# Hybrid DiT step in split fp32: loads and products of the start reordered, the last unit's second stream in two fresh banks, later gate rows and residual, other tables

## The chip, the cores and the metric

The kernel runs on one core of one Trainium2 chip. The metric is the device time in microseconds of one execution. A core has five engines that run their own instruction streams side by side: TensorE (PE, matrix products into PSUM banks), VectorE (DVE), ScalarE (ACT), GpSimd (POOL) and SyncE (SP, which here issues most DMAs). They wait for each other by semaphores.

## What is computed

One layer of a diffusion backbone for 128 prompt tokens and 128 sample tokens, model width 2048, all in fp32:

```python
shift1, scale1, gate1, shift2, scale2, gate2 = split(silu(c) @ w_ada + b_ada, 6)   # adaLN, per stream
h  = rms_norm(x) * (1 + scale1) + shift1
qa, ka, va, qb, kb, vb, ga, gb = split(h @ w_in)                                   # 2048 x 8704
oa = window_gqa(qa, ka, va, cache_a)       # 8 heads of 128, 2 key/value heads, rotary, QK-norm
ob = neighbourhood(qb, kb, vb, cache_b)    # 8 heads of 128, 2-D bias, QK-norm
m  = (sigmoid(ga) * (oa @ w_br_a) + sigmoid(gb) * (ob @ w_br_b)) @ w_out
x  = x + gate1 * m
h2 = rms_norm(x) * (1 + scale2) + shift2
y  = x + gate2 * (relu(h2 @ w_up) ** 2 @ w_down)                                   # inner width 8192
```

The new keys and values of the prompt are outputs too.

## The kernel before

**Products.** Every fp32 operand is split into a high part, which the engine multiplies in one pass, and a low rest; a product is the sum of three matmuls, high x high, high x low and low x high (L467 to L469 and L340 to L342, and L1408 to L1410 in the fast pairs). ACT makes a weight's high part by a copy (L108). The low part is made in one of two ways: DVE subtracts the high part from the raw weight (L268), or `minus_plus` (L274, L275) lets ACT write the negative of the high part and POOL issue a DMA that adds the raw weight from memory onto it. Tables choose the second way: `LO_DMA` for plain weights (wL), `XL_DMA` and `YL_DMA` for two halves of a fast pair (XL, YB); their keys are step numbers, or 8 times the piece plus the place in it.

**Steps.** The weights go by in steps of 512 KB (128 x 1024 values): SP loads a step into a buffer `raw` (L239), ACT and DVE split it, PE multiplies it in 12 matmuls of 512 columns, six for each of the two token streams (0 is the prompt, 1 the sample), into two PSUM banks. A unit is a run of steps that ends in one pair of banks, 512 output columns wide. `run()` walks all steps; at each it issues loads, splits and products so many steps ahead as the tables `RUN`, `LOOK` and `AHEAD` say. Other work is hung onto steps by tables (`ADA_AT`, `JOBS`, `POST`, `DOTS`, `T_PAIR` and more).

**The start.** The first five steps are written out by hand in `begin()` (L530 to L690): their loads go in halves of 256 KB (`k` is the half), between the loads of the first two adaLN pairs (`pair_load`, L349). The rest of the adaLN products goes through `mod_pairs`: groups 1 to 6 of eight loads each (`araw`) and their products (`ps_ada`, L358), at the steps in `ADA_AT`.

**Attention.** Probabilities are transposed either by PE (L963, for the entries of `TE`) or by DMA.

**The MLP.** The up-projection runs in pieces; where `FAST` names them, pairs of blocks go through a scheme with one product fewer, on sums of blocks (`up_pair`, L1408 to L1521). The down-projection's partial sums of a piece wait in `dsum`, some of them in memory (`DS_AWAY`), and are put back into a bank by ACT.

**The end.** The last unit of all is `last_unit` (L1338): for its last two steps it computes stream 0 first, evacuates it (`out_s`: DVE multiplies by the gate rows, L1138, and adds to the residual x1b, L1142; SP stores), and then finishes stream 1, its last step in two halves of 256 columns in the same bank. The gate rows g2 and the residual (`gate_bc`, `x1_back`) are loaded ahead, six steps before the end of a unit of the piece before the last.

Of the kernel before, what the change touches and what calls it, by code (L numbers as in the profile page):

```python
# [32 lines left out]
SILU_AT = 6  # L33
FB_DVE = 6
FB1 = 14
H_AT = 42
DOTS1 = [19, 26, 29, 33, 34, 34, 40, 42]
# [12 lines left out]
BEGIN_SEED = ()  # L50
FAST = {1: (0, 1, 3, 7), 2: (0, 2, 4, 7), 3: (0, 3, 4, 5, 7), 4: (0, 2, 4, 6, 7), 5: (0, 1, 3, 6, 7), 6: (0, 1, 3, 6, 7), 7: (0, 2, 3, 5, 7)}
AWAY = [('gB', 2), ('gB', 0), ('gA', 0)]
GATE_BACK = 7
SEED_IN = {3: 0, 4: 1}
SEED_AT = 4
DIRECT = (3,)
LO_DMA = {123: 3, 162: 4, 196: 6, 205: 8, 233: 5, 421: 5, 452: 5}

LOOK = "220102342600004321112333333423344346003343323264425550024766435445100474621316521154444204744421242145443452135211233544444376555544342442445533113321545566643343457745545676631233475557402456897561133345442776554653214434322546645533234767635734543210333332754523544642203425555547355455542235444454346622143243143533120323340312252123324443413423323622444434555345666437402100223322544523544524557200014130212545432212544243022242111444300005772000137786"
RUN = "143538999224623021111226444342023133100001316655554435733333554564563325525103544635357136486300020025420321354421003432333255533612243352667454523663311454555543535997565577799967554203545745166866764795556988745674676472100044367288985999944454243112133555665422126411011224421346635244575533444454353423332446683456501300223410454545542322431521552123100123853233511252576696622311441202144625734434231022445134778334434464132124568676567978669999987788"  # L60
AHEAD = "822111111111101110000000111111110000000000122222221000000000000011122211000020133110000100000233100000000000002200000000000001112000000000000111000000100000000000000000011100000011111232221244332110000000000000000000000003011311110000000002000000000001020000000000000000000000000000002220001100100000000000000000000000000100000000000000001000222222222322320000000000000000000010000000000100000000000000000000000000000211110000000100000000012444242132345400"
CONST_AT = [63, 75]
XL_DMA = {9: 0, 11: 11, 16: 0, 20: 8, 23: 6, 26: 0, 29: 0, 36: 0, 37: 0, 38: 0, 43: 0, 46: 5, 53: 0, 54: 0, 63: 0}
ADA_G = ((1,), (2,), (3, 4), (5, 6))
ADA_AT = [None, 5, 14, 20, 22, 37, 38]
# [8 lines left out]
DOTS2 = [222, 233, 234, 234, 235, 238, 245, 247, 254, 265, 269, 270, 272, 288, 300, 301, 304, 327, 328, 331, 333, 336, 349, 359, 360, 362, 364, 368, 393, 393, 395, 401]
STAT_AT = [4, -1, 9, 3]
T_PAIR = [[12, 6], [6, 10], [5, 10], [6, 10], [6, 10], [6, 10], [7, 12]]
P_PAIR = [[3, -1], [2, 4], [3, 3], [1, 4], [2, 5], [1, 5], [2, 0]]
# [9 lines left out]
def tile_hybrid_step(ctx: ExitStack, tc: tile.TileContext, a):  # L87
# [10 lines left out]
    def G(name, dt=F32):  # L98
        return gp.tile([P, 1024], dt, name=name, tag="g")
# [427 lines left out]
    def begin():  # L527
# [21 lines left out]
        def lo(j, k):  # L549
            prep_lo(sts[j], k)  # L550
# [65 lines left out]
        for j in range(2, n):  # L616
            banks(j)
            if 3 < j + 1 < n:
                hi(j + 1, 0)
                lo(j + 1, 0)  # L620
            if j == n - 2:
                mod_q(1, 2)
            by_stream(j, 0, 0)
            if j == n - 2:
                mod_q(1, 3)
                ada_evac(mb[1], 256)
            if j == n - 1:
                first_h(1)
                hi(1, 1)
            keep(j, 0)  # L630
            by_stream(j, 0, 1)
            if j == n - 2:
                ada_cols(mb[1], 0, 1, 1)
                hi(0, 1)
                lo(0, 1)
            keep(j, 1)
# [701 lines left out]
    def last_unit(w, c0, ktiles, stat, evac_s, key, seed_from=None):  # L1338
# [207 lines left out]
    def down_unit(p, n):  # L1546
# [261 lines left out]
```

## Time and profile before

| | before |
|---|---|
| median of 3 runs | 1321.33 us (1320.77 to 1322.04) |
| the profiled run | 1321.1 us, span 1319.3 us |
| PE busy | 1306.7 us, 99% of the span |
| DVE busy | 1123.5 us, 85% |
| ACT busy | 905.1 us, 69% |
| moved by DMA | 400.12 MB, mean 303 GB/s |

The span is the profiled time from the first to the last instruction. An engine's busy time counts overlapping matmuls once. PE's clock was granted in full in all of the 40 slices of the page.

### The profile page before, as it was taken

How to read it: one execution, taken by the hardware profiler on the slowest of the kernel's cores; microseconds unless marked ns; L12 is line 12 of the kernel's file. 1: busy time of each engine (PE TensorE's matmuls, PEld its weight loads, DVE VectorE, ACT ScalarE, POOL GpSimd, SP SyncE). 2: the span in 40 equal slices, each digit the busy share in tenths (PEclk: the TensorE clock that was granted, in tenths of full speed). 3: DMA queues.
4: the chain of work that ended last, by engine and by line, in shares of the span. 5: the costliest groups of instructions: out<-in, count | busy, mean ns of one | idle time of the engine just before them, and what ended most of it. 6: DMA issues, size and time to landing. Idle time of an engine off the chain costs nothing. (4 is left out here: it accounts for less than half of the span.)

```text
span 1319.3 us, 18022 instructions
## 1 busy us (share of the span) xinstructions
PE 1306.7 (99%) x6334; PEld 1057.9 (80%) x6335; DVE 1123.5 (85%) x1437; ACT 905.1 (69%) x1143; POOL 57.1 (4%) x65
## 2 busy tenths in 40 slices
PE   9999999999999999999999999999999999999998
PEld 4778778788888878888888888888888778878887
DVE  4669799988999999999788897997999899879474
ACT  5635655789866556536786868869778597787780
POOL 0000000431000000001000000000000000000000
PEclk9999999999999999999999999999999999999999
DMA  9999999998899989988798998778896886788861
GB/s 374 408 408 371 409 409 354 395 289 262 281 339 314 407 308 330 374 332 254 235 259 308 290 324 256 275 263 252 279 321 222 272 279 240 254 274 299 303 263 48
DMA packets 168939, 400.12 MB, mean 303 GB/s; under 512 B 70768, under 2 KB 72016, under 8 KB 168848
## 3 DMA queue, kind: packets, MB, share of 16 engines
q1 hardware_dynamic: 164688, 387.09, 81.3%
q0 software_dynamic: 4016, 11.80, 4.8%
q8 instruction: 49, 0.80, 0.2%
q14 instruction: 42, 0.34, 0.1%
q10 hardware_dynamic: 144, 0.08, 0.0%
HBM read 373.45 MB, written 10.80 MB: 291 GB/s over the span
## 5 line engine op out<-in xcount | busy, mean ns | idle before, releaser
L268 DVE TENSOR_TENSOR wL<-raw,wH 128x1024 fp32r<-128x1024 f32 x382 | 450.8, 1221 | 79.1 <-ACT wH L108 71.3
L108 ACT ACTIVATE wH<-raw 128x1024 fp32r<-128x1024 f32 (+1 forms) x396 | 393.2, 1040 | 107.5 <-DMA raw<-in_w_in 20.9
L467 PE MATMUL acc<-wH,hH 128*128 128x512 f32 x272 | 107.5, 395 | 0.6 <-ACT wH L108 0.6
L468 PE MATMUL acc<-wL,hH 128*128 128x512 f32 x272 | 105.9, 390 | 0.0
L469 PE MATMUL acc<-wH,hL 128*128 128x512 f32 x272 | 105.9, 389 | 0.0
L340 PE MATMUL acc<-wH,hH 128*128 128x512 f32 x252 | 100.7, 399 | 0.0
L342 PE MATMUL acc<-wH,hL 128*128 128x512 f32 x252 | 98.2, 390 | 0.0
L341 PE MATMUL acc<-wL,hH 128*128 128x512 f32 x252 | 98.2, 390 | 0.0
L1638 DVE CUSTOM_DVE_ANT_0 aT<-aT,cB,cols 128x1024 f32<-128x1024 f32 x56 | 71.5, 1283 | 0.6
L1638 DVE CUSTOM_DVE_ANT_0 junk<-aT,cB,cols 128x1024 bf16<-128x1024 f32 x56 | 71.5, 1284 | 0.0
L108 ACT ACTIVATE uH<-raw 128x1024 fp32r<-128x1024 f32 x33 | 35.1, 1063 | 45.0 <-DVE raw L1473 35.4
L467 PEld LDWEIGHTS acc<-wH,hH 128*128 128x128 f32 x272 | 51.1, 188 | 15.2 <-issue 2.9
L469 PEld LDWEIGHTS acc<-wH,hL 128*128 128x128 f32 x272 | 51.1, 188 | 10.8
L468 PEld LDWEIGHTS acc<-wL,hH 128*128 128x128 f32 x272 | 51.1, 188 | 10.1
L340 PEld LDWEIGHTS acc<-wH,hH 128*128 128x128 f32 x252 | 47.4, 188 | 10.4 <-issue 0.9
L341 PEld LDWEIGHTS acc<-wL,hH 128*128 128x128 f32 x252 | 47.4, 188 | 10.0 <-issue 0.5
L342 PEld LDWEIGHTS acc<-wH,hL 128*128 128x128 f32 x252 | 47.3, 188 | 9.9
L108 ACT ACTIVATE tH<-t 128x1024 fp32r<-128x1024 f32 x33 | 35.0, 1060 | 26.6 <-DVE t L1465 26.4
L1465 DVE TENSOR_TENSOR t<-raw 128x1024 f32<-128x1024 f32 x33 | 40.2, 1219 | 3.4 <-PE acc L342 2.3
L108 ACT ACTIVATE fTa<-pTa 128x2048 uint16<-128x2048 uint16 x16 | 40.6, 2535 | 1.5 <-DMA pTa<-pla 1.5
L1521 ACT ACTIVATE up<-up 128x1024 f32<-128x1024 f32 x28 | 29.7, 1062 | 17.1 <-DVE up L1511 16.7
L1476 DVE TENSOR_TENSOR uL<-raw,uH 128x1024 fp32r<-128x1024 f32 x33 | 40.4, 1225 | 0.9
(684 smaller groups left out, 3335.4 us busy)
## 6 DMA issues: line engine op xcount, KB each, us to landing
raw<-in_w_in SPq DMA_DIRECT2D x131, 512.0 KB, 9.0
raw<-in_w_down SPq DMA_DIRECT2D x128, 512.0 KB, 7.2
araw<-in_w_pair SPq DMA_DIRECT2D x80, 512.0 KB, 10.2
raw<-in_w_upF SPq DMA_DIRECT2D x66, 512.0 KB, 5.7
aT<-in_w_gT SPq DMA_DIRECT2D x64, 512.0 KB, 8.4
raw<-in_w_up SPq DMA_DIRECT2D x62, 512.0 KB, 6.0
aT<-in_w_adaT SPq DMA_DIRECT2D x48, 512.0 KB, 8.6
raw<-in_w_out SPq DMA_DIRECT2D x32, 512.0 KB, 8.9
```

The costliest lines, as they stand in the source:

```text
L108: act.activation(out, in_, AF.Copy)
L268: dve.tensor_tensor(st["lo"], st["raw"], st["hi"].bitcast(F32), op=OP.subtract)
L340: pe.matmul(acc[tb], sh, wh[:, k, :], start=f, stop=False, **kw)
L341: pe.matmul(acc[tb], sh, wl[:, k, :], start=False, stop=False, **kw)
L342: pe.matmul(acc[tb], sl, wh[:, k, :], start=False, stop=l, **kw)
L467: pe.matmul(acc[tb], sh, wh[:, k, :], start=kt == 0 and k == 0 and not held and not seeded, stop=False, **kw)
L468: pe.matmul(acc[tb], sh, wl[:, k, :], start=False, stop=False, **kw)
L469: pe.matmul(acc[tb], sl, wh[:, k, :], start=False, stop=last and k == 1 and not hold, **kw)
L1465: dve.tensor_tensor(t.rearrange("p (a n) -> p a n", a=2), X.rearrange("p (a n) -> p a n", a=2), Y[:, 0:512].unsqueeze(1).to_broadcast([P, ...
L1476: dve.tensor_tensor(b["uL"], Y, b["uH"].bitcast(F32), op=OP.subtract)
L1521: act.activation(u.rearrange("p s n -> p (s n)"), u.rearrange("p s n -> p (s n)"), f)
L1638: dve.tensor_tensor_reduce(out, box["raw"], cB[s, tag], 1.0, dst if second else baT[:, part, fb:fb + 1], OP.mult, OP.add, dst)
```

## The change

- `begin()`: the loads stand in another order (first adaLN pair, first halves of steps 0 to 2, second pair, first halves of steps 3 and 4, all second halves), and so do the products: step 2 comes ahead of the second pair's products, which now stand in one row, and steps 3 and 4 behind them.
- `last_unit`: stream 1's steps but the last two are added to the residual early (`add_s`); its last two steps go in halves of 256 columns into two fresh banks, all 12 matmuls of one half first.
- `gate_bc` and `x1_back` of g2 are loaded nine steps ahead of the end of the unit that uses them, in the last piece.
- `TE` loses one of four entries. `DS_AWAY` has five entries and not seven, `AWAY` two and not three.
- By the tables 37 low halves are made by accumulating DMA and not 25: XL 15 for 12, YB 16 for 10, wL 6 for 3. Three of seven rows of `FAST` name other places, the same number of them.
- Many tables that place work have other numbers. Of them the diff shows some.

```diff
@@ tables @@
-TE = (('A', 0, 0), ('A', 0, 1), ('qA', 1), ('qB', 1))
-DS_AWAY = [0, 1, 2, 9, 13, 20, 22]
+TE = (('A', 0, 0), ('qA', 1), ('qB', 1))
+DS_AWAY = [0, 1, 9, 20, 22]
-YL_DMA = [11, 15, 16, 23, 27, 31, 38, 39, 48, 56]
+YL_DMA = [11, 15, 16, 18, 20, 23, 24, 27, 28, 31, 32, 38, 39, 48, 54, 56]
+G2_LEAD = 9
-ADA_LD = [1, 0, 0, 2, 1, 0, 0]
+ADA_LD = [-2, 1, 0, 0, 0, 0, 0]
-AWAY = [('gB', 2), ('gB', 0), ('gA', 0)]
-GATE_BACK = 7
+AWAY = [('gB', 3), ('gB', 0)]
+GATE_BACK = 0
-ADA_AT = [None, 5, 14, 20, 22, 37, 38]
+ADA_AT = [None, 5, 14, 20, 22, 37, 40]
...
@@ begin @@
-        for k in range(2):
-            pair_load(mb[k], 0, k)
-            for st in sts:
-                if k == 0:
-                    st["raw"], st["mm"], st["prep"] = G("raw"), lambda st: None, lambda: None
-                sync.dma_start(st["raw"][:, halves[k]], st["src"][:, halves[k]])
+        pair_load(mb[0], 0, 0)
+        for j in range(3):
+            half_load(j, 0)
+        pair_load(mb[1], 0, 1)
+        for j in range(3, n):
+            half_load(j, 0)
+        for j in range(n):
+            half_load(j, 1)
...
-        mod_q(1, 0)
         rest(1, 0)
+        banks(2)
+        for tb in range(2):
+            by_stream(2, 0, tb)
+            keep(2, tb)
+        for q in range(4):
+            mod_q(1, q)
         hi(3, 0)
         lo(3, 0)
-        mod_q(1, 1)
...
+        ada_evac(mb[1], 256)
+        hi(4, 0)
+        banks(3)
+        by_stream(3, 0, 0)
+        ada_cols(mb[1], 0, 1, 1)
+        lo(4, 0)
+        first_h(1)
...
@@ last_unit @@
                 if q < n - 2:
-                    mms(q, 1)
+                    mms(q, 1, end=n - 3)
+                if q == n - 3:
+                    add_s(box["acc"], 1)
                 if q == n - 1:
                     evac_s(box["acc"], 0)
-                    mms(q - 1, 1)
-                    for c in (slice(0, 256), slice(256, 512)):
-                        mms(q, 1, c)
-                        evac_s(box["acc"], 1, c)
+                    box["acc"] = [None, bank("acc"), bank("acc")]
+                    for i, c in enumerate((slice(0, 256), slice(256, 512))):
+                        for qq in (q - 1, q):
+                            mms(qq, 1, c, 1 + i, q - 1)
+                        evac_s(box["acc"][i:], 1, c)
@@ g2 rows and residual @@
-        e = end_of(("down", last - 1, n))
-        load_at(e - 6, lambda n=n: gate_bc("g2", n))
-        load_at(e - 6, lambda n=n: x1_back(n))
+        e = end_of(("down", last, n)) - G2_LEAD
+        load_at(e, lambda n=n: gate_bc("g2", n))
+        load_at(e, lambda n=n: x1_back(n))
```

How instructions stand on three engines, before and after. On SP's queue, the loads of adaLN groups 5 and 6 (`araw`, eight each), with weight steps (`raw`) and rows for DVE's dot products (`aT`) between them, before:

```order
L349 DMA araw<-in_w_pair 128x1024 x8
L239 DMA raw<-in_w_in 128x1024
L349 DMA araw<-in_w_pair 128x1024 x8
L239 DMA raw<-in_w_in 128x1024
L1627 DMA aT<-in_w_adaT 128x1024
```

and after:

```order
L350 DMA araw<-in_w_pair 128x1024 x8
L240 DMA raw<-in_w_in 128x1024 x2
L1643 DMA aT<-in_w_adaT 128x1024
L240 DMA raw<-in_w_in 128x1024
L350 DMA araw<-in_w_pair 128x1024 x8
L240 DMA raw<-in_w_in 128x1024
```

Between the two groups four loads stand where one stood.

On ACT, the high copies of the fast pair of key 18 (XH, YB) and what follows them, before:

```order
L274 ACTIVATE XL_7101<-XH_7099 128x1024
L108 ACTIVATE XH_7150<-raw_6911 128x1024
L108 ACTIVATE YB_7164<-raw_6948 128x512
L108 ACTIVATE tH_7166<-t13_7170 128x1024
L108 ACTIVATE uH_7168<-raw_6948 128x1024
```

and after:

```order
L275 ACTIVATE XL_7100<-XH_7098 128x1024
L109 ACTIVATE wH_7147<-raw_7075 128x1024
L109 ACTIVATE YB_7161<-raw_7073 128x512
L275 ACTIVATE YB_7161<-YB_7161 128x512
L109 ACTIVATE tH_7163<-t13_7167 128x1024
L109 ACTIVATE uH_7165<-raw_7073 128x1024
```

The copy of YB is followed by its negative, which before stood there for XL of key 20 alone, and a weight's high copy stands where XH stood.

On PE, the end of the program, the last unit's two last steps (wH and wL are the parts of a weight step, the first name is the bank), before:

```order
L1353 MATMUL acc_11598<-wH_11540,a15L_11348 128x512
L1351 MATMUL acc_11599<-wH_11538,a15H_11347 128x512
...
L1353 MATMUL acc_11599<-wH_11538,a15L_11348 128x512
L1351 MATMUL acc_11599<-wH_11540,a15H_11347 128x256
...
L1353 MATMUL acc_11599<-wH_11540,a15L_11348 128x256
L1351 MATMUL acc_11599<-wH_11540,a15H_11347 128x256
...
L1353 MATMUL acc_11599<-wH_11540,a15L_11348 128x256
```

and after:

```order
L1365 MATMUL acc_11594<-wH_11626,a15L_11340 128x512
L1363 MATMUL acc_11693<-wH_11531,a15H_11339 128x256
...
L1363 MATMUL acc_11693<-wH_11626,a15H_11339 128x256
...
L1365 MATMUL acc_11693<-wH_11626,a15L_11340 128x256
L1363 MATMUL acc_11694<-wH_11531,a15H_11339 128x256
...
L1363 MATMUL acc_11694<-wH_11626,a15H_11339 128x256
...
L1365 MATMUL acc_11694<-wH_11626,a15L_11340 128x256
```

Before, the sample stream has six matmuls of 512 columns and two groups of six of 256 columns, all in one bank; now it has two groups of twelve of 256 columns, each in a bank of its own.

## Rows read from the trace of the kernel before

**Rows 1.** The page: busy us, share of the span, instructions of each engine.

```profile
PE 1306.7 (99%) x6334; PEld 1057.9 (80%) x6335; DVE 1123.5 (85%) x1437; ACT 905.1 (69%) x1143; POOL 57.1 (4%) x65
```

**Rows 2.** Waits of PE: waiting group <- releaser, total us, times, longest.

```profile
PE acc L340 <- ACT acc L108: 1.6, 2, 1.2
PE ps_ada L358 <- DMA araw<-in_w_pair: 1.5, 2, 1.0
...
PE Q L1409 <- DMA XL<-in_w_upF: 0.9, 1, 0.9
PE Q L1409 <- DMA YB<-in_w_upF: 0.9, 1, 0.9
```

**Rows 3.** Timeline of the last unit: start, us, engine, line, shape, [idle before <- releaser].

```profile
1310.96 0.39 PE L1353 MATMUL acc<-wH,a15L 128*128 128x512 f32 x1
...
1311.19 0.39 PE L1351 MATMUL acc<-wH,a15H 128*128 128x512 f32 x1
...
1311.39 0.69 DVE L1138 TENSOR_TENSOR t<-g,acc 128x512 f32<-128x512 f32 x1 [5.13 <-PE acc L1353]
...
1312.55 0.28 PE L1351 MATMUL acc<-wH,a15H 128*128 128x256 f32 x1
...
1313.14 0.28 PE L1353 MATMUL acc<-wH,a15L 128*128 128x256 f32 x1
1313.46 0.42 DVE L1138 TENSOR_TENSOR t<-g,acc 128x256 f32<-128x256 f32 x1 [0.66 <-PE acc L1353]
...
1313.93 0.39 PE L1351 MATMUL acc<-wH,a15H 128*128 128x256 f32 x1 [0.52 <-DVE t L1138]
...
1314.95 0.42 DVE L1138 TENSOR_TENSOR t<-g,acc 128x256 f32<-128x256 f32 x1 [0.61 <-PE acc L1353]
```

**Rows 4.** Timeline of PE, products of adaLN group 6.

```profile
149.66 3.23 PE L358 MATMUL ps_ada<-araw,cpad 128*32 128x256 f32 x56
153.37 0.64 PE L358 MATMUL ps_ada<-araw,cpad 128*32 128x256 f32 x8 [0.48 <-DMA araw<-in_w_pair]
```

**Rows 5.** Timeline of PE, the first four of the eight probability transposes.

```profile
298.04 0.60 PE L963 MATMUL ps_PT<-ident,prob 128*128 128x128 f32 x4
298.47 0.94 PE L913 MATMUL ps_S<-T_kvA,T_qA 128*128 128x128 f32 x7
```

**Rows 6.** Timeline of PE in the start: two places where it waited.

```profile
19.75 0.64 PE L358 MATMUL ps_ada<-araw,cpad 128*32 128x256 f32 x8 [1.04 <-DMA araw<-in_w_pair]
...
36.42 0.47 PE L467 MATMUL acc<-wH,hH 128*128 128x512 f32 x1 [0.63 <-ACT wH L108]
```

**Rows 7.** Busy time of each engine in a stretch of the start.

```profile
20.00:30.00 10.00, 9.98 (x62) 5.66 (x55) 3.56 (x10) 5.88 (x13) 0.00 (x0) 1.00 1.03 402
```

**Rows 8.** Accumulating DMAs into YB: POOL's issue, ns; time to landing.

```profile
L275 POOL DMA_DIRECT2D YB<-in_w_upF x10: 847/854/857, 687.0 to 1179.8; - x10
...
DMA to landing us min/median/max: 3.7/6.5/8.4
```

**Rows 9.** The same for XL.

```profile
L275 POOL DMA_DIRECT2D XL<-in_w_upF x12: 847/855/882, 663.7 to 1213.7; - x12
...
DMA to landing us min/median/max: 5.2/6.0/10.9
```

**Rows 10.** Timeline near three YB: high copies, first products, one negative copy and issue.

```profile
766.87 0.61 ACT L108 ACTIVATE YB<-raw 128x512 fp32r<-128x512 f32 x1
...
774.73 0.39 PE L1408 MATMUL Q<-YB,h20H 128*128 128x512 f32 x1
...
924.20 0.62 ACT L108 ACTIVATE YB<-raw 128x512 fp32r<-128x512 f32 x1
...
931.81 0.39 PE L1408 MATMUL Q<-YB,h20H 128*128 128x512 f32 x1
...
1178.90 0.63 ACT L274 ACTIVATE YB<-YB 128x512 fp32r<-128x512 f32 x1
...
1179.83 0.86 POOL L275 DMA_DIRECT2D YB<-in_w_upF  x1 [56.50 <-ACT YB L274]
```

More of the change, by code (lines that the diff above doesn't have):

```diff
@@ L35 @@
 FB1 = 14
-H_AT = 42
-DOTS1 = [19, 26, 29, 33, 34, 34, 40, 42]
+H_AT = 36
+DOTS1 = [18, 26, 29, 33, 34, 34, 40, 42]
 CHUNKS = [2, 2, 2, 4, 6]
@@ L43 @@
 EXTRA = (('gB', 0),)
[L44 to L45 removed]
+TE = (('A', 0, 0), ('qA', 1), ('qB', 1))
+DS_AWAY = [0, 1, 9, 20, 22]
 DS_BACK = 6
[L47 removed]
+YL_DMA = [11, 15, 16, 18, 20, 23, 24, 27, 28, 31, 32, 38, 39, 48, 54, 56]
 PREP_LATE = 9
[L49 removed]
+G2_LEAD = 9
+ADA_LD = [-2, 1, 0, 0, 0, 0, 0]
 BEGIN_SEED = ()
[L51 to L53 removed]
+FAST = {1: (0, 1, 3, 7), 2: (0, 2, 4, 7), 3: (0, 3, 4, 5, 7), 4: (0, 1, 4, 6, 7), 5: (0, 1, 3, 6, 7), 6: (0, 2, 5, 6, 7), 7: (0, 1, 3, 5, 7)}
+AWAY = [('gB', 3), ('gB', 0)]
+GATE_BACK = 0
 SEED_IN = {3: 0, 4: 1}
@@ L62 @@
-CONST_AT = [63, 75]
-XL_DMA = {9: 0, 11: 11, 16: 0, 20: 8, 23: 6, 26: 0, 29: 0, 36: 0, 37: 0, 38: 0, 43: 0, 46: 5, 53: 0, 54: 0, 63: 0}
+LO_DMA = {192: 12, 205: 8, 219: 9, 229: 3, 355: 5, 402: 6, 421: 4, 453: 6, 455: 3}
+LOOK = "243120121611115310223432224545455446003343323375535550002544235445000474622316521154444204744443242145443452135211033544444376555524342442445433113321545566643342457634434788853455586457402456897561133125442776554653214434322546645533234767634734543210333332754523544662203536555547465566542235444434346620143243144643122323340312252123324443413423323622444434556345844437412100223322554523544524557200014130012545432333653354122352211434300115762211148776"
@@ L64 @@
+CONST_AT = [67, 73]
+XL_DMA = {9: 0, 11: 10, 15: 6, 16: 0, 19: 6, 20: 8, 24: 0, 26: 0, 29: 5, 36: 0, 37: 0, 38: 6, 40: 5, 43: 0, 46: 5, 53: 0, 54: 0, 62: 8, 63: 0}
 ADA_G = ((1,), (2,), (3, 4), (5, 6))
-ADA_AT = [None, 5, 14, 20, 22, 37, 38]
-XS_AT = {1: 9, 2: 24, 3: 37}
-POST = {('kvA', 0): [66, 70, 73], ('qA', 0): [65, 71, 75, 75, 77], ('qA', 1): [70, 74, 75, 76, 82], ('kB', 0): [74, 77, 79, 83, 85], ('qB', 0): [81, 82, 86, 88, 90], ('kB', 1): [84, 88, 91, 92, 97], ('qB', 1): [89, 92, 99, 100, 101]}
@@ L68 @@
-JOBS = [[79, 80, 82, 83, 85, 86, 89], [81, 83, 84, 86, 87, 92, 99], [86, 86, 87, 89, 91, 91, 106], [91, 92, 93, 96, 99, 105, 111], [93, 97, 99, 101, 101, 104, 115], [96, 101, 102, 104, 106, 106, 115], [106, 106, 108, 110, 117, 118, 125], [109, 111, 116, 117, 119, 123, 125]]
+ADA_AT = [None, 5, 14, 20, 22, 37, 40]
+XS_AT = {1: 5, 2: 24, 3: 38}
+POST = {('kvA', 0): [66, 70, 73], ('qA', 0): [65, 71, 75, 75, 77], ('qA', 1): [70, 75, 75, 80, 82], ('kB', 0): [74, 77, 79, 80, 85], ('qB', 0): [81, 82, 86, 88, 90], ('kB', 1): [84, 86, 91, 92, 97], ('qB', 1): [88, 93, 99, 100, 100]}
@@ L69 @@
+JOBS = [[79, 80, 81, 86, 88, 89, 92], [81, 83, 84, 86, 88, 92, 101], [86, 86, 87, 89, 90, 90, 103], [91, 91, 93, 93, 93, 105, 110], [93, 95, 99, 101, 102, 104, 115], [96, 101, 102, 104, 106, 106, 115], [106, 106, 108, 110, 119, 122, 125], [109, 111, 115, 117, 119, 123, 124]]
 SS_G = [(0, 2), (2, 1)]
-SS_AT = [50, 53, 71, 73, 131, 141]
+SS_AT = [50, 53, 68, 73, 127, 141]
 T_AT = [3, 4]
-PREP_IN = [6, 8]
-DOTS = [33, 43, 47, 49, 50, 51, 52, 54, 56, 56, 56, 56, 60, 62, 63, 67, 70, 73, 80, 84, 89, 91, 92, 93, 96, 98, 102, 103, 104, 106, 108, 109, 109, 112, 114, 117, 118, 120, 122, 122, 126, 126, 129, 129, 129, 131, 132, 137, 138, 138, 140, 144, 145, 146, 154, 155, 156, 160, 160, 163, 167, 169, 173, 173, 175, 175, 179, 179, 180, 182, 184, 190]
@@ L74 @@
[L74 to L77, printed above, removed]
+PREP_IN = [5, 7]
+DOTS = [38, 47, 47, 49, 50, 51, 52, 54, 56, 56, 56, 56, 60, 62, 63, 67, 70, 73, 80, 84, 89, 91, 92, 93, 96, 98, 102, 103, 104, 106, 108, 109, 109, 112, 114, 117, 118, 120, 122, 122, 123, 126, 129, 129, 129, 131, 132, 137, 138, 138, 140, 144, 145, 146, 155, 155, 156, 160, 160, 163, 167, 169, 173, 173, 175, 175, 179, 179, 180, 182, 184, 189]
@@ L78 @@
+DOTS2 = [219, 230, 233, 233, 235, 238, 245, 247, 253, 269, 269, 270, 271, 291, 300, 301, 304, 327, 328, 331, 333, 336, 349, 359, 360, 362, 364, 368, 393, 393, 395, 401]
+STAT_AT = [2, 0, 10, 2]
+T_PAIR = [[11, 5], [6, 10], [5, 10], [4, 10], [8, 10], [6, 10], [8, 12]]
+P_PAIR = [[3, -1], [1, 2], [3, 3], [1, 4], [3, 5], [0, 5], [2, 0]]
 M_TE = (3,)
@@ L80 @@
 FLIP = 1
-P_UP = [3, 3]
-T_UP = [16, 11]
+P_UP = [1, 3]
+T_UP = [18, 11]
 COL = {"qA": 0, "kvA": 1024, "qB": 1536, "kB": 2560, "vB": 3584, "gA": 4608, "gB": 6656}
@@ L532, in begin, with half_load @@
         halves = [slice(512 * k, 512 * k + 512) for k in range(2)]
-        for k in range(2):
-            pair_load(mb[k], 0, k)
-            for st in sts:
-                if k == 0:
-                    st["raw"], st["mm"], st["prep"] = G("raw"), lambda st: None, lambda: None
-                sync.dma_start(st["raw"][:, halves[k]], st["src"][:, halves[k]])
+        def half_load(j, k):
+            st = sts[j]
+            if k == 0:
+                st["raw"], st["mm"], st["prep"] = G("raw"), lambda st: None, lambda: None
+                st.pop("load")
+            sync.dma_start(st["raw"][:, halves[k]], st["src"][:, halves[k]])
+        pair_load(mb[0], 0, 0)
[6 more added lines that the diff above has]
+            half_load(j, 1)
         loads.sort(key=lambda x: x[:2])
@@ L610, in begin @@
         lo(2, 0)
-        mod_q(1, 0)
         rest(1, 0)
+        banks(2)
[4 more added lines that the diff above has]
+            mod_q(1, q)
         hi(3, 0)
         lo(3, 0)
-        mod_q(1, 1)
[L616 to L628, printed above, removed]
-                hi(1, 1)
[L630 to L636, printed above, removed]
+        ada_evac(mb[1], 256)
[5 more added lines that the diff above has]
+        first_h(1)
+        keep(3, 0)
+        by_stream(3, 0, 1)
+        hi(0, 1)
+        lo(0, 1)
+        keep(3, 1)
+        banks(4)
+        for tb in range(2):
+            by_stream(4, 0, tb)
+            if tb == 0:
+                hi(1, 1)
+            keep(4, tb)
         lo(1, 1)
@@ L1336, in up_unit, with last_unit @@
         at(end_of(("up", n)) + T_UP[n], lambda: up_T(n))
-    def last_unit(w, c0, ktiles, stat, evac_s, key, seed_from=None):
+    def last_unit(w, c0, ktiles, stat, evac_s, add_s, key, seed_from=None):
         box = {"hl": {}}
@@ L1343, in last_unit, with mms @@
             at(len(wsteps) - SEED_AT, lambda: seed(box, seed_from()))
-        def mms(q, tb, c=slice(0, 512)):
+        def mms(q, tb, c=slice(0, 512), to=None, begin_=0, end=n - 1):
             wh, wl = box["hl"][q]
@@ L1348, in mms @@
                 sh, sl = stat(q // 2)(2 * (q % 2) + k, tb)
-                kw = {"skip_group_check": True} if seed_from else {}
-                acc = box["acc"][tb][:, c]
-                pe.matmul(acc, sh, wh[:, k, c], start=q == 0 and k == 0 and not seed_from, stop=False, **kw)
+                seeded = seed_from and not begin_
+                kw = {"skip_group_check": True} if seeded else {}
+                acc = box["acc"][tb if to is None else to][:, c]
+                pe.matmul(acc, sh, wh[:, k, c], start=q == begin_ and k == 0 and not seeded, stop=False, **kw)
                 pe.matmul(acc, sh, wl[:, k, c], start=False, stop=False, **kw)
-                pe.matmul(acc, sl, wh[:, k, c], start=False, stop=q == n - 1 and k == 1, **kw)
+                pe.matmul(acc, sl, wh[:, k, c], start=False, stop=q == end and k == 1, **kw)
         for j, k0 in enumerate(ktiles):
@@ L1567, in down_unit @@
         if p == last and n == 3:
-            last_unit(a["w_down"], 512 * n, [4 * j for j in PIECES[p]], stat, lambda acc, s, *c: out_s(acc, n, s, *c), ("down", p, n),
+            last_unit(a["w_down"], 512 * n, [4 * j for j in PIECES[p]], stat, lambda acc, s, *c: out_s(acc, n, s, *c),
+                      lambda acc, s: resid("g2", acc[s], n, s), ("down", p, n),
                       (lambda: dsum.pop(n)) if seeded else None)
@@ L1715, in tile_hybrid_step @@
     for n in range(4):
-        e = end_of(("down", last - 1, n))
-        assert i + 6 < e
-        load_at(e - 6, lambda n=n: gate_bc("g2", n))
-        load_at(e - 6, lambda n=n: x1_back(n))
+        e = end_of(("down", last, n)) - G2_LEAD
+        assert i + 3 < e
+        load_at(e, lambda n=n: gate_bc("g2", n))
+        load_at(e, lambda n=n: x1_back(n))
     e = end_of(("out", 3))
```

6 lines of the change are left out of this document (2 added, 4 removed).

## Prediction

> **What bounds the kernel now.** I read the page first. TensorE (PE) is busy for 99% of a span of 1319.3 us, VectorE (DVE) for 1123.5 us and ScalarE (ACT) for 905.1 us [rows 1]. So the time is PE's instructions plus the few places where PE stands still; work taken from DVE or ACT is worth nothing by itself. The second view is PE's waits [rows 2]: two accumulator seeds by ACT 1.6 us together, the adaLN pair loads 1.5, a low weight half XL that comes by accumulating DMA 0.9, and one YB of that kind 0.9. The third view is the timeline at these places. In the last unit PE waits 0.52 us for a DVE multiplication that reads the bank into which PE wants to write [rows 3]. In adaLN group 6, the last of the large ones, it waits 0.48 us for a load [rows 4]. At the start there are 1.04 us for a load and 0.63 us for ACT [rows 6]. All waits that can be seen come to some 6 us, about half a per cent of the time.
>
> The profiled run took 1321.1 us, 1.8 us more than its span; the median of the runs is 1321.33. I add up against the profiled run and put the difference onto the median.
>
> **The change part by part.**
>
> *The last unit.* Before, the prompt stream's last matmul starts at 1310.96, then six full matmuls of the other stream (1311.19 to 1312.55, so 0.227 us each) and two halves of six 256-column matmuls, which go into one bank. The halves are 0.118 us apart (1312.55 to 1313.14 are five steps). The second half can't start until DVE has read the first: PE waits until 1313.93, and the last multiplication starts at 1314.95 [rows 3]. After, 24 halves stand in a row, the first twelve for one fresh bank, the others for a second. By the same step the 24th starts at 1311.19 + 23 x 0.118 = 1313.90. DVE follows 0.32 us behind (as 1313.46 does behind 1313.14), so at 1314.22 and not at 1314.95: **-0.73 us**. DVE is free by then: its multiplication of the prompt stream (1311.39, 0.69 us) and an add of the same width end near 1312.8, when the first twelve halves are done (1311.19 + 11 x 0.118 + 0.32 = 1312.81), and the two operations of 0.42 us on them end near 1313.7. The extra pair of 512-wide operations lies before 1311.39, where DVE had been idle for 5.13 us. If they came at the end they would cost 1.4 us. Bounds: -0.52 (only the wait goes) to -0.8.
>
> *adaLN group 6.* Its table entry goes from step 38 to 40, so its products come two steps later; a step is 12 matmuls of 0.227 us, so 5.4 us. In the load queue four loads and not one now stand between group 5's loads and its own, three more. Loads here land one behind the other: 512 KB at 402 GB/s [rows 7] are 1.3 us, so the last quarter lands 3.9 us later. It was 0.48 us late [rows 4]; it will be 5.4 - 3.9 - 0.48 = 1.0 us early: **-0.5 us**. Bounds 0 (if the queue slips by another 1.0 us) to -0.65 with the slow restart behind the wait.
>
> *Four transposes leave PE.* The first four of the eight probability transposes take 298.04 to 298.47 [rows 5]: **-0.43 us**. They become DMA transposes with two copies and one join on ACT, hidden as long as ACT runs ahead of PE. If PE came to wait for the join, the gain would be lost; bounds -0.43 to +0.5.
>
> *The start.* The loads of the second pair of adaLN group 0 now stand ahead of the first halves of weight steps 3 and 4, 256 KB each. The pair so lands 1.3 us earlier, and its products come later in PE's order: the wait of 1.04 us at 19.75 goes [rows 6]. But the two halves land four loads, 5.2 us, later, and ACT, which splits them, was busy for only 5.88 of these 10 us [rows 7], so it can take up 4.1 us of that and be up to 1.1 us late. The next stop of PE, at 36.42, is released by ACT [rows 6]. What PE saves ahead of it is then waited for there, unless ACT's queue ends earlier too, and that it does not: it gets the same pieces, two of them later. I put this at **0**, between -1.7 (both waits go) and +1.1.
>
> *Low halves by accumulating DMA.* Twelve more of the low halves (3 XL, 6 YB, 3 wL) are made by a negative copy on ACT and an accumulating DMA that POOL issues, twelve fewer by a DVE subtraction. DVE loses these subtractions and ACT gains as many copies; neither is a gain or a cost as long as it stays hidden. What counts is the way from ACT's high copy to the DMA's landing: a negative copy of 0.63 us, 0.30 us until POOL issues (1178.90 + 0.63 to 1179.83) [rows 10], and for YB 3.7, 6.5 or 8.4 us to the landing (least, median, most), for XL 5.2, 6.0 or 10.9 [rows 8, 9]. For the YB at 766.87 the high copy ends at 767.48, so the median way ends at 774.91. PE's first product on it starts at 774.73, and the one that takes the low half one step later, at 774.96: just in time at the median, 1.9 us late at the longest. For the one at 924.20 the same sum gives 932.25 against 932.04, 0.2 us late at the median and 2.1 at the longest [rows 10]. A third YB (key 20) has about the same lead. One XL (key 53) stands as close to its use in ACT's order as any. The other new ones have more room. Before, 2 of the 22 XL and YB halves made PE wait, each 0.9 us [rows 2]. With four that are close, I bound the cost by 0 and 4 x 0.9 = 3.6 us and take **+0.5 us**, near the median way.
>
> The Trainium skill, page "DMA: Bandwidth & Descriptors", section "Anatomy of one DMA — SWDGE (gpsimd) path", gives 2.0 us plus the bytes at 436 GB/s, for these 256 KB 2.6 us. Not one of the ten YB here was that fast: 3.7 at the least [rows 8]. By the page's price this term would be 0 and the sum 0.5 us lower; the measured landing decides.
>
> *Without a price.* Fewer spills (two sums, one gate) and later loads of the last gate rows and residual shift traffic on the load queue, which stands full at the start alone. The eight loads come nine steps ahead of their use, 24 us. The other tables move work of DVE and ACT between steps: 0, with unknown ends on both sides, which I put at 1 us.
>
> Sum: -0.73 - 0.5 - 0.43 + 0 + 0.5 = **-1.2 us**, from 1321.1 to 1319.9, on the median 1320.1.
>
> **The rivals.**
>
> *More waits go than I counted.* The seeds (1.6 us), the XL and the YB of before (0.9 each) [rows 2] and the start (up to 1.7) hang on the order on ACT and the load queue, and the tables move both. For: most of these waits are short beside the shifts. Against: the YB and that XL keep their places in ACT's order relative to PE. If all go and nothing comes: 1321.33 - 1.7 - 5.1 = 1314.5; half of them give 1317.0.
>
> *Low halves come late: slower.* One mechanism, at the four close ones. If they take the longest landing times of the rows, PE waits 1.9, 2.1, about 1.7 for the third and as much for the XL, 7.4 us: 1321.33 - 1.7 + 7.4 = 1327. It decides from 4.3 us of new waits on, that is 1.1 us each; below that the gains cover them. For: two of 22 were late already. Against: the longest landing is rare.
>
> *POOL can't write its descriptors while DVE works.* If each of the four close ones had to wait for one of DVE's subtractions, 1.22 us, this would be 4.9 us: 1321.33 - 1.7 + 4.9 = 1324.5. Against it: POOL's issue takes 847, 854 and 857 ns at least, median and most in ten cases, with DVE busy for 85% of the span [rows 1, 8]; nothing there is held up. The Trainium skill says on the page "SBUF — State Buffer", section "Who interferes with whom", that a DMA which GpSimd issues can be starved of the port for its descriptors by a DVE operation that holds it; this speaks against more such DMAs, and the trace of before doesn't bear it out.
>
> *It does not do what it says.* Group 6's load or the transposes' join is late by as much as it saves, and new waits eat the tail: 1321.3.
>
> **How the numbers follow.** A measurement of this kernel can tell about 0.2%, 2.6 us, from no change: faster is below 1318.7, slower above 1324.0. Chances: forecast 1320.1 (1318.7 to 1321.0) 0.40; more waits go, 1317.0, 0.31; no effect, 1321.3, 0.14; low halves late 0.13; POOL held up 0.02. Most of the second case is below 1318.7 and a little of the forecast too: faster 0.33. Slower 0.14, same 0.53. The range: the second case reaches from 1314.5 to 1318.7, and a cut at 1316.3 leaves out about 0.1 of the chance; above, the bound of 3.6 us on the late halves gives 1321.33 - 1.66 + 3.6 = 1323.3, and what lies beyond is the third case.
>
> **What would show it right or wrong.** The last unit: the wait on the multiplication gone and the last multiplication 3.3 us after the start of the prompt stream's last matmul rather than 4.0 us. Group 6: no wait of PE in the products near 153 us. The start: no wait near 19.75, and a wait on ACT near 36 that is larger than 0.63 us; if that is smaller, my 0 is wrong. The low halves: XL or YB by DMA in PE's waits at up to four new places, under 1.1 us each. The forecast is wrong if the seeds' 1.6 us vanish or if a DVE subtraction, which releases no wait of a main product now, begins to do so.

## The result

The changed kernel takes 1323.24 us (median of ten runs, 1321.52 to 1326.51), the kernel before in the same comparison 1320.95 (1319.34 to 1322.24). The ratio is 1.0021, with a 95% interval of 1.0011 to 1.0031: about 2.8 us slower, where I had forecast 1.2 us faster. The profiled execution of the changed kernel is the longest of its ten, 1326.5 us with a span of 1324.7 (another took 1326.3); this has to be kept in mind when its waits are added up.

The profile after. First the page's engines, which answer to [rows 1]:

```profile
PE 1307.4 (99%) x6337; PEld 1059.1 (80%) x6337; DVE 1115.5 (84%) x1427; ACT 915.4 (69%) x1156; POOL 66.2 (5%) x77
```

DVE has 8 us less to do and ACT 10 us more; neither is what the time is made of. PE's waits, which answer to [rows 2] (waiting group <- releaser, total us, times, longest):

```profile
PE Q L1424 <- DMA YB<-in_w_upF: 6.1, 3, 2.8
PE Q L1424 <- DMA XL<-in_w_upF: 1.2, 1, 1.2
...
PE acc L570 <- ACT wH L109: 1.0, 2, 0.7
...
PE acc L342 <- DVE wL L269: 0.5, 1, 0.5
```

The two seeds with their 1.6 us are gone, and so is the last unit's wait. In their place PE waits for YB by accumulating DMA at three places and not one, 6.1 us against 0.9. Where, the timeline shows (start, us, engine, line, shape, [idle before <- releaser]); these are the fast pairs of keys 18 and 32 of [rows 10]:

```profile
768.01 0.63 ACT L275 ACTIVATE YB<-YB 128x512 fp32r<-128x512 f32 x1
...
768.94 0.86 POOL L276 DMA_DIRECT2D YB<-in_w_upF  x1 [1.27 <-ACT YB L275]
...
775.24 0.39 PE L1423 MATMUL Q<-YB,h20H 128*128 128x512 f32 x1
...
777.39 0.50 PE L1424 MATMUL Q<-YB,h20H 128*128 128x512 f32 x1 [1.77 <-DMA YB<-in_w_upF]
...
936.23 0.50 PE L1424 MATMUL Q<-YB,h20H 128*128 128x512 f32 x1 [1.47 <-DMA YB<-in_w_upF]
```

For key 18 POOL issues at 768.94, PE could use the low half at 775.24 + 0.23 = 775.47, and PE waits 1.8 us for it. The third is key 56, which was late before too, by 0.9 us. Here it is late by 2.84, and something comes on top (timeline of PE, then busy time of PE, PEld, DVE, ACT, POOL, granted clock, DMA share, GB/s by stretch):

```profile
1189.36 0.39 PE L1423 MATMUL Q<-YB,h20H 128*128 128x512 f32 x1
1192.59 0.80 PE L1424 MATMUL Q<-YB,h20H 128*128 128x512 f32 x1 [2.84 <-DMA YB<-in_w_upF]
1193.18 0.63 PE L1425 MATMUL Q<-YB,h20L 128*128 128x512 f32 x1
1193.61 0.63 PE L1423 MATMUL Q<-tH,sH 128*128 128x512 f32 x1
...
1195.74 0.51 PE L1425 MATMUL Q<-uH,sL 128*128 128x512 f32 x1
1196.09 0.39 PE L1423 MATMUL Q<-tH,sH 128*128 128x512 f32 x1
```

```profile
1186.00:1189.00 3.00, 3.00 (x15) 2.49 (x14) 2.90 (x5) 1.53 (x4) 0.00 (x0) 1.00 0.98 362
...
1193.00:1197.00 4.00, 4.00 (x12) 3.13 (x12) 3.96 (x5) 2.95 (x4) 0.00 (x0) 0.63 1.03 423
```

Matmuls that start 0.23 us apart elsewhere start 0.43 us apart from 1193.18 on, until 1195.74. The granted clock of this stretch is 0.63 and not 1.00: after 2.84 us without work PE ran at the lower of its two levels, 1.2 and not 2.4 GHz, for a while. From 1192.59 to 1196.09 eight matmuls took 3.50 us and not 1.81: 1.7 us more than the wait itself. Key 56 was so late because its lead was short: from POOL's issue to PE's use there were 4.8 us, and 6.65 in the kernel before, while the DMA took 7.8 us and 7.6. What made ACT late stands further up in its timeline:

```profile
1169.23 1.06 ACT L109 ACTIVATE wH<-raw 128x1024 fp32r<-128x1024 f32 x1 [3.33 <-DMA raw<-in_w_down]
```

ACT waited 3.33 us for a weight's load. In the twelve other traces no such wait near this place is over 0.7 us, so it belongs to this execution. It is probably part of why this one is 3.3 us above the median; what the other long executions waited for no trace shows.

The last lines answer to [rows 3, 4, 6]: the end, group 6 and the start.

```profile
1317.61 0.39 PE L1365 MATMUL acc<-wH,a15L 128*128 128x512 f32 x1
...
1320.59 0.28 PE L1365 MATMUL acc<-wH,a15L 128*128 128x256 f32 x1
1320.90 0.42 DVE L1149 TENSOR_TENSOR t<-g,acc 128x256 f32<-128x256 f32 x1 [0.56 <-PE acc L1365]
```

```profile
155.56 3.66 PE L359 MATMUL ps_ada<-araw,cpad 128*32 128x256 f32 x64
```

```profile
21.45 2.02 PE L359 MATMUL ps_ada<-araw,cpad 128*32 128x256 f32 x32
24.18 0.50 PE L570 MATMUL acc<-wH,hH 128*128 128x512 f32 x1 [0.71 <-ACT wH L109]
```

### The profile page after: what moved, and what is told of

Read it like the earlier page. It is cut to its first block, busy times and chain, and to the rows that moved or that the text cites. A ratio compares the mean times of both kernels' runs of the same rounds, so it can differ in the third digit from the quotient of the medians.

```text
span 1324.7 us, 18044 instructions
## 1 busy us (share of the span) xinstructions
PE 1307.4 (99%) x6337; PEld 1059.1 (80%) x6337; DVE 1115.5 (84%) x1427; ACT 915.4 (69%) x1156; POOL 66.2 (5%) x77
## 4 chain that ended last, share of the span: by engine, by line
PE 82%; DMA 8%; ACT 4%; issue 3%; DVE 3%; SPq 0%; DVEq 0%; ACTq 0%; POOLq 0%; POOL 0%
PE acc L342 14%; PE acc L341 14%; PE acc L343 14%; PE Q L1424 6%; PE Q L1425 6%; PE Q L1423 6%; PE acc L468 4%; PE acc L469 4%; PE acc L470 4%; DMA raw<-in_w_in 2%; DMA YB<-in_w_upF 2%; PE ps_ada L359 2%; DVE wL L269 1%; DMA araw<-in_w_pair 1%; ACT wH L109 1%
```

## The experiments

Two theories. **A**: the loss is the accumulating DMAs that land after their use, above all the three new ones at keys 18, 20 and 32; the rest of the change gains about what I had summed up. **B**: the loss is the other tables' order, and the late YB of the trace are that execution's. Ratios are to the kernel before on the same chip, with 95% intervals.

**Only the late halves, put into the kernel before.**

```diff
-YL_DMA = [11, 15, 16, 23, 27, 31, 38, 39, 48, 56]
+YL_DMA = [11, 15, 16, 18, 20, 23, 27, 31, 32, 38, 39, 48, 56]
```

> The kernel before, with the low halves of three YB (keys 18, 20 and 32) made by a negative copy and an accumulating DMA instead of a DVE subtraction; nothing else. Theory A (the accumulating DMAs of 18 and 32 land after their use): PE waits at both, about 1.5 to 2 us each, key 20 waits 0 to 1 us; the time rises by 2.5 to 4 us over before, to 1323.5 to 1325. Rival B (the loss of the change lies in the other tables' order, and the waits on YB of its profile are that one execution's): less than 0.6 us over before.

Measured: 1323.03 us against 1321.35, ratio 1.0017 (1.0008 to 1.0026), +2.2 us. That three numbers of one table make the kernel before as slow as the changed one speaks for A, though the rise and both waits are smaller than A expected, and it rules out that the waits were one execution's. The waits in its timeline:

```profile
776.05 0.50 PE L1409 MATMUL Q<-YB,h20H 128*128 128x512 f32 x1 [0.58 <-DMA YB<-in_w_upF]
...
934.36 0.50 PE L1409 MATMUL Q<-YB,h20H 128*128 128x512 f32 x1 [0.92 <-DMA YB<-in_w_upF]
```

Key 20 costs nothing that can be seen there. Each wait is smaller than in the changed kernel, and so is the sum. Other waits differ as well: XL 43 takes 1.4 us and not 0.9, and the seeds 0.2 and not 1.6. The seeds can't be counted as won back, for in the seven traces of kernels with all seven spills they take anything from 0.2 to 1.6 us.

**The changed kernel without them.**

```diff
-YL_DMA = [11, 15, 16, 18, 20, 23, 24, 27, 28, 31, 32, 38, 39, 48, 54, 56]
+YL_DMA = [11, 15, 16, 23, 24, 27, 28, 31, 38, 39, 48, 54, 56]
```

> The changed kernel, with the low halves of YB 18, 20 and 32 back on DVE; nothing else. Theory A: the waits at 777 and 936 us of the changed kernel's trace go, the time falls by 2.5 to 4 us below the changed kernel's 1323.2, to 1319.3 to 1320.7, at or a little under before. Rival B: it stays within 0.6 us of 1323.2, or DVE, which gets three subtractions back, makes PE wait in their place.

Measured: 1319.12 us, ratio 0.9984 (0.9976 to 0.9993), 2.1 us below before. So the three cost the changed kernel 4.9 us (1.0021 - 0.9984 of 1321, some 2 us to either side by the two intervals), and B falls. Of these, 3.2 us are the waits at keys 18 and 32 in its trace; where the rest goes is not shown. The late ones that are left:

```profile
PE Q L1424 <- DMA XL<-in_w_upF: 1.8, 2, 1.6
PE Q L1424 <- DMA YB<-in_w_upF: 1.2, 1, 1.2
```

**Without any that was late.** YB 20 stays with the DMA.

```diff
-YL_DMA = [11, 15, 16, 18, 20, 23, 24, 27, 28, 31, 32, 38, 39, 48, 54, 56]
+YL_DMA = [11, 15, 16, 20, 23, 24, 27, 28, 31, 38, 39, 48, 54]
-XL_DMA = {..., 40: 5, 43: 0, 46: 5, ...}
+XL_DMA = {..., 40: 5, 46: 5, ...}
```

> The changed kernel, with the low halves of YB 18, 32 and 56 and of XL 43 by DVE, so of all four that PE waited for in its profile; YB 20 stays with the DMA. Theory A: no wait of PE on XL or YB is left over 0.3 us, the time is 1316.5 to 1319, below both kernels. Rival B: 1322 or more.

Measured: 1315.97 us (five runs, 1314.81 to 1317.65), ratio 0.9961 (0.9949 to 0.9973), 5.2 us below before: it beats both kernels. A expected at least 1316.5, so it was even a little better; that no wait on XL or YB would be over 0.3 us was a miss, XL 36 has 0.5. PE's waits that are left behind the start, from 60 us on:

```profile
PE acc L342 <- DVE wL L269: 0.9, 1, 0.9
...
PE acc L468 <- ACT acc L109: 0.6, 1, 0.6
...
PE Q L1424 <- DMA XL<-in_w_upF: 0.5, 1, 0.5
```

**One more.** XL 36, on which the 0.5 us are spent, by DVE too.

```diff
-XL_DMA = {..., 29: 5, 36: 0, 37: 0, ...}
+XL_DMA = {..., 29: 5, 37: 0, ...}
```

> The changed kernel with the low halves of YB 18, 32 and 56 and of XL 43 and 36 by DVE: one more than in the version with four, whose trace had one wait of 0.5 us left on XL 36. If DVE covers this one too: -0.5 us, 1315.5. If DVE is by now late itself, PE waits for a DVE subtraction instead and the time is 1316 or more.

Measured: 1315.66 us, ratio 0.9964 (0.9950 to 0.9977). By its trace no wait on XL or YB is left; by the time it can't be told from the version with four. It is the other version that beats both kernels.

**The same cure for the kernel before**: YB 56 and XL 43 by DVE.

```diff
-YL_DMA = [11, 15, 16, 23, 27, 31, 38, 39, 48, 56]
+YL_DMA = [11, 15, 16, 23, 27, 31, 38, 39, 48]
-XL_DMA = {..., 38: 0, 43: 0, 46: 5, ...}
+XL_DMA = {..., 38: 0, 46: 5, ...}
```

> The kernel before with the low halves of YB 56 and XL 43 by DVE, nothing else. Both waits (0.9 us each in its profile) should go: -1.8 us, to 1319.5. With this the rest of the change is read: the changed kernel without its late halves ran at 1316.0, so the rest would be worth -3.5 us. Rival: what is saved at 1031 us is given back at the seeds at 1057 us, where ACT waits for a load, and only -0.9 us is left.

Measured: 1318.36 us, ratio 0.9982 (0.9973 to 0.9990), -2.4 us; the rival's -0.9 lies outside. Against the version with four by DVE (0.9961) the rest of the change is worth 2.8 us, not 3.5; with the two intervals some 1 to 5 us.

**An earlier place for the copies.** Can the DMA way be saved by an earlier start?

```diff
 LOOK[250] 1 -> 3
 LOOK[308] 3 -> 5
 LOOK[404] 4 -> 5
```

> The changed kernel with three numbers of LOOK raised, so that the fast pairs of keys 18, 32 and 56 are split two steps (5.4 us of matmuls) earlier; their YB low halves still come by accumulating DMA. If what counts is the lead of ACT's negative copy over PE (my theory), the waits on YB 18 and 32 shrink from 1.8 and 1.5 us to under 0.5, that on 56 too, and the time falls by 3 to 5 us below the changed kernel, to 1318 to 1320. If the accumulating DMA is simply late by its place in the queues (rival), or ACT waits for the raw weights so that the earlier place brings no earlier copy, the waits stay within 0.5 us of what they were and the time at 1322.5 or more.

Measured: 1322.39 us, ratio 1.0017 (1.0008 to 1.0026). My expectation missed: keys 18, 32 and 56 still wait 1.4, 1.3 and 1.0 us. ACT's timeline ahead of key 32 tells why there:

```profile
918.94 2.55 ACT L109 ACTIVATE fTa<-pTa 128x2048 uint16<-128x2048 uint16 x1
...
922.49 1.99 ACT L109 ACTIVATE wH<-raw 128x1024 fp32r<-128x1024 f32 x2
...
926.95 0.64 ACT L275 ACTIVATE YB<-YB 128x512 fp32r<-128x512 f32 x1
```

ACT works here without a gap: a join of 2.55 us, weight copies, an accumulator's evacuation, then the pair's copies. The new place stands earlier in the table, but ACT's order ahead of it stays the same, and ACT is not idle: the negative copy starts at 926.95, and in the changed kernel, 0.6 us later all along, at 927.52. So a table number is no lead where ACT is the bound. That ACT waited for the raw weights, as my rival had it, isn't so at this place. At key 18 it is different:

```profile
767.69 0.86 POOL L276 DMA_DIRECT2D YB<-in_w_upF  x1 [0.32 <-DVE gc_g L1654]
...
774.93 0.39 PE L1423 MATMUL Q<-YB,h20H 128*128 128x512 f32 x1
776.70 0.50 PE L1424 MATMUL Q<-YB,h20H 128*128 128x512 f32 x1 [1.38 <-DMA YB<-in_w_upF]
```

The lead grew there, from 6.53 to 774.93 + 0.23 - 767.69 = 7.47 us, but the DMA took 9.0 us and not 8.4, so that most of the 0.9 us was lost again: that is the other rival, a DMA that is late by its place. That other places would do was not tried.

**The last unit alone** (the diff of the change's `last_unit`).

> The kernel before with the changed last unit alone (the second stream's last two steps in halves in two fresh banks, its first part added to the residual early). By my sum -0.7 us against before, by the distance from the first stream's last matmul to the end of the span in the two profiles -1.2 us (8.3 against 7.1 us). Rival: the end is set by the output stores, and the time does not move (within 0.2 us).

Measured: 1320.55 us, ratio 0.9993 (0.9984 to 1.0001), -0.9 us with an interval that just takes in none. The trace is sharper:

```profile
1312.41 0.39 PE L1354 MATMUL acc<-wH,a15L 128*128 128x512 f32 x1
...
1315.39 0.28 PE L1354 MATMUL acc<-wH,a15L 128*128 128x256 f32 x1
1315.71 0.42 DVE L1138 TENSOR_TENSOR t<-g,acc 128x256 f32<-128x256 f32 x1 [0.56 <-PE acc L1354]
```

From the prompt stream's last matmul to the last multiplication it is 3.30 us, and before it was 3.99. The rest that the changed kernel gains at its end (2.9 us from the last add to the end of the span, 3.5 in the kernel before and here) doesn't come from this unit; its cause stays open.

**The start alone** (the diff of the change's `begin`).

> The kernel before with the changed start alone (loads and products of the first five steps in the other order). My term was 0 (between -1.7 and +1.1); the two profiles say -0.2 us at the first product behind the start. Rival: the saved wait of 1.0 us counts in full, -1.0 us.

Measured: 1320.33 us, ratio 0.9996 (0.9987 to 1.0004): no change that can be told, and by the time alone the rival's -1.0 us isn't excluded. PE's waits in its start:

```profile
PE acc L569 <- ACT wH L108: 1.0, 2, 0.7
...
PE acc L467 <- ACT wH L108: 0.6, 1, 0.6
PE acc L571 <- DVE wL L258: 0.6, 2, 0.3
```

The 1.04 us for the load are gone, and 1.0 us for ACT and 0.6 us for DVE stand there now, for the weights whose halves come later; the 0.63 us near 36 stay as they were. That speaks against the rival.

**One spill fewer.**

```diff
-DS_AWAY = [0, 1, 2, 9, 13, 20, 22]
+DS_AWAY = [0, 1, 2, 9, 20, 22]
```

> The kernel before with one spill fewer: the sum of piece 3, block 1 (entry 13 of DS_AWAY) is not put into memory and taken back, whose 512 KB come back in the load queue right ahead of the weight loads for which ACT waits at 1055 us. If that reload makes the seeds late, PE's wait on the seeds (1.6 us) goes and the time is 1319.3 to 1320; if the wait has another cause, it stays at 1.3 to 1.6 us and the time within 0.5 us of before.

Measured: 1320.58 us, ratio 0.9995 (0.9986 to 1.0004). PE's wait on the seeds is gone, and for the load on which ACT waited 2.60 us in the kernel before it waits less:

```profile
1053.66 1.06 ACT L108 ACTIVATE wH<-raw 128x1024 fp32r<-128x1024 f32 x1 [0.68 <-DMA raw<-in_w_down]
```

It is one trace, and in four others, with this spill still in, ACT waited there at most 1.14 us and PE 0.2 to 0.4 us on the seeds. So the trace agrees with the reload as the cause, but what the spill is worth is less sure: 0.2 to 1.6 us. And the time hardly moves. In the trace the YB of key 56 takes 0.8 us more:

```profile
1178.29 0.85 POOL L275 DMA_DIRECT2D YB<-in_w_upF  x1 [56.51 <-ACT YB L274]
```

```profile
PE Q L1409 <- DMA YB<-in_w_upF: 1.7, 1, 1.7
```

PE comes to that place 1.5 us earlier, and so does POOL's issue (1178.29 against 1179.83 in [rows 10]); but this time the DMA took 8.5 us to land and not 7.6.

**The adaLN tables alone**, in one run.

```diff
-ADA_LD = [1, 0, 0, 2, 1, 0, 0]
+ADA_LD = [-2, 1, 0, 0, 0, 0, 0]
-ADA_AT = [None, 5, 14, 20, 22, 37, 38]
+ADA_AT = [None, 5, 14, 20, 22, 37, 40]
```

> The kernel before with the changed tables of the adaLN groups alone (ADA_AT and ADA_LD). By my sum PE's wait in group 6 (0.48 us) goes and a load is 1.0 us early. The trace decides: no wait on the adaLN loads near 153 to 159 us if the step holds; if the queue slips, a wait of 0.3 to 0.8 us at the new place near 159 us. The time can't tell half a microsecond.

Measured: 1321.02 us in one run against 1320.26, within the spread. The products of group 5 and 6 are one row without a wait between:

```profile
156.24 3.66 PE L358 MATMUL ps_ada<-araw,cpad 128*32 128x256 f32 x64
```

The 1.7 us on adaLN loads that it still shows are 1.1 at the start and 0.6 at an earlier group near 102 us, whose entry these tables move as well: alone, they put the wait elsewhere.

**The four transposes alone**, in one run.

```diff
-TE = (('A', 0, 0), ('A', 0, 1), ('qA', 1), ('qB', 1))
+TE = (('A', 0, 0), ('qA', 1), ('qB', 1))
```

> The kernel before with four probability transposes moved from PE to DMA alone (TE). By my sum PE has 0.43 us less to do near 298 us. If ACT's two copies and one join were hidden, PE stays 0.4 us ahead of before behind this point; if ACT is the bound there, a weight's low half comes late near 311 us and PE waits 0.4 to 1.0 us for DVE, as it did in the changed kernel (0.5 us), and the gain is lost.

Measured: 1326.31 us in one run against 1320.26. Neither of my two cases:

```profile
PE ps_S L913 <- ACT prob L938: 3.4, 1, 3.4
```

```profile
329.85 1.38 ACT L108 ACTIVATE fTPA<-pTPA 128x1024 uint16<-128x1024 uint16 x1 [5.99 <-DMA pTPA<-plPA]
```

With the old `JOBS` the attention's next scores wait 3.4 us for the bank that ACT has not read yet, because ACT stood at the new join for 5.99 us until the transposing DMA had landed. The change has other numbers in `JOBS` and has no such wait, on PE or on ACT. The wait on DVE near 311 us is not in this trace.

## Why the prediction was wrong

**What failed is one term: the low halves by accumulating DMA, +0.5 us.** Three of these twelve halves alone cost the changed kernel 4.9 us, and the kernel before 2.2 (1.1 to 3.4). Of the four that I had called close, keys 18 and 32 made PE wait; key 20 and XL 53 did not.

At these two the lead was right. For key 18 I had 774.96 - (767.48 + 0.63 + 0.30) = 6.55 us from POOL's issue to the use; in the changed kernel it is 775.47 - 768.94 = 6.53. (At key 20 it was not: 6.7 us in the kernel before, 11.2 in the changed one, where the copy comes earlier and PE, after its wait at key 18, later; so its landing of 8.1 us did no harm.)

The landing was not right. I took the median of all ten YB, 6.5 us, as if they were draws from one distribution. They are not: as long as the program around it stays, a place repeats. The DMA issues at two places, kernel before (out<-in, queue, KB, us to landing; keys 16 and 23, at 753.69 and 789.48 us):

```profile
YB<-in_w_upF POOLq DMA_DIRECT2D x1, 256.0 KB, 7.7
...
YB<-in_w_upF POOLq DMA_DIRECT2D x1, 256.0 KB, 8.4
```

and the kernel with the three halves, another execution of nearly the same program, at the same places:

```profile
YB<-in_w_upF POOLq DMA_DIRECT2D x1, 256.0 KB, 7.8
...
YB<-in_w_upF POOLq DMA_DIRECT2D x1, 256.0 KB, 7.9
```

These repeat within half a microsecond, and over all ten places the two traces differ by 0 to 1.1 us. With the changed tables the times are others. The changed kernel at keys 18, 23 and 32:

```profile
YB<-in_w_upF POOLq DMA_DIRECT2D x1, 256.0 KB, 8.4
...
YB<-in_w_upF POOLq DMA_DIRECT2D x1, 256.0 KB, 4.0
...
YB<-in_w_upF POOLq DMA_DIRECT2D x1, 256.0 KB, 7.7
```

The half of key 23 takes 7.6 to 8.4 us in all eight traces of the kernel before and its versions, and 4.0 to 5.1 in all five of the changed kernel and its versions; that of key 15 goes the other way, from 3.8 to 4.2 up to 7.0 to 7.3. So no row of the old trace gave the price.

The nearest YB to key 18, one on each side, were 7.7 and 8.4; with 8.0 the sum would have been 1.5 us late for 18 alone, but by luck, since these two neighbours land after 6.1 and 4.0 us in the changed kernel. The nearest to key 32 were 6.2 and 6.8, which would have said half a microsecond late at most, and PE waited 1.47. My own case of the longest landing, 1.9 and 2.1 us late, was the nearest to what came. What sets the time of a place is not shown by these runs. The median of 6.5 stood for places from 3.7 to 8.4. The bound of 3.6 us (four at 0.9) was too low for the same reason: the 0.9 is what two places happened to be late by, no price for another place.

**The rivals.** What happened is the third case, the low halves that come late, near its point of decision: 4.9 us of cost at three halves against the 4.3 that I had named. I gave it 0.13. I had counted two late ones in 22 as a frequency, though what decides is each one's lead against its own landing. The case that POOL is held up by DVE is not it: POOL's issue in the changed kernel, and the landing times (ns and us, min/median/max):

```profile
L276 POOL DMA_DIRECT2D YB<-in_w_upF x16: 865/865/867, 687.5 to 1184.8; - x16
...
DMA to landing us min/median/max: 4.0/7.1/8.4
```

865 to 867 ns in sixteen cases leaves no room for a wait of POOL within its issue. The rule of the Trainium skill (page "SBUF — State Buffer", section "Who interferes with whom") is not seen at work here, and no run here has a DVE operation beside these DMAs that would test it sharply. The estimate of 2.6 us by the Trainium skill, page "DMA: Bandwidth & Descriptors", section "Anatomy of one DMA — SWDGE (gpsimd) path", is too low here by 1.4 us at the quickest landing and by 4.5 at the median.

**The other steps.**

- Last unit, -0.73: right. 3.29 us from the prompt stream's last matmul to the last multiplication (1317.61 to 1320.90), and 3.30 with this part alone.
- Start, 0: the size fits (-0.5 us for this part alone, -1.7 to +0.5), and what is saved is waited for again, but not where I had it. The wait at 19.75 is gone; 0.71 us for ACT at 24.18 and smaller ones up to 29.43, 1.55 us together, stand there instead. The wait on ACT near 36 is 0.64 us, no larger than before, which I had named as a sign against my 0.
- Group 6, -0.5: right at its place. Of the 1.0 us by which I had the load early, little is left: one other version of the changed kernel waited 0.44 us there, three did not.
- Transposes, -0.43: PE has the work no more, but the cover that I named, ACT ahead of PE, is thin. PE waits 0.5 us for a DVE subtraction near 311 us, 0.8 and 0.9 in the versions with fewer late halves, behind ACT's weight copies; the gain is lost there. I had named such a wait as a sign of a wrong forecast. That the transposes are the cause of it is not shown: alone in the kernel before they bring no such wait, and `JOBS` and `POST` have other numbers too.
- "Without a price": wrong in one point. I had left the seeds' waits as they were, and named their going as a sign of a wrong forecast. They are in all seven traces with the seven spills and in none of the six without that of piece 3, block 1, whose sum came back in the load queue just ahead of the weight for which ACT waited. What that is worth is between 0.2 and 1.6 us by the traces, and not to be told by the time.
- The sum without the low halves was -1.7 us; the changed kernel without the three is at -2.1 (-3.2 to -0.9). That the total fits is in part luck: the seeds were missing in it on one side and the wait near 311 us on the other.

## What to carry to other kernels

Here a DMA's time to land belonged to its place in one schedule, and was not a draw from all DMAs of its kind; when the tables changed, the same half took 4 us less or 3 us more. So neither a median nor the neighbours of an old trace price a new DMA: compare its lead with the longest landing seen, place by place, and read the landing from a trace of the new program. Work that was moved off an engine with slack onto a path with a latency gained nothing here and cost its lateness; DVE had the time for the five halves that were given back to it. And a wait that is taken away can come back at the next place, as the 0.5 us for XL 36 did: look what is late next, before the gain is counted.

## What the runs showed of the hardware

Two things I hadn't expected. The landing times repeat by place as long as the tables stay, and move with them: at key 23 they are 7.6 to 8.4 us in eight traces and 4.0 to 5.1 in five. And a wait of PE of 2.84 us cost 1.7 us more than itself, since the granted clock fell to the lower level behind it (0.63 over the stretch 1193 to 1197, matmuls 0.43 us apart). The wait of 3.35 us in the version with the transposes alone shows it too: matmuls 0.43 us apart and a granted clock of 0.50 from 335.5 to 338.8 us. Behind the waits of 1.77 and 1.47 us in the changed kernel's trace the granted clock is 1.00.
